# Second conv matrix of a hybrid decoder layer: half of its columns by the seven-product scheme, with three sums of weights made by transfers

## Chip, cores and metric

One NeuronCore of one Trainium2 chip. The metric is the device time of one execution in microseconds (us), as the median of several runs. Of the kernel before there are three runs, from 1184.03 to 1184.84 us, median 1184.58 us.

## What is computed

One layer over 256 tokens (and 16 learned ones in front of them), width D = 2048, all in float32. The part that matters here is the mixer's second branch and what follows it:

```python
u = rms_norm(h, g_pre_mix[l])
z_pool, v_conv, g_conv, gate_a, gate_b = jnp.split(u @ w_in[l], splits, axis=-1)
y_a = causal_multiscale_pool(z_pool, ...) @ w_pool_out[l]
y_b = conformer_conv(v_conv, g_conv, ...) @ w_conv_out[l]      # (256 x 1024) @ (1024 x 2048)
m = jax.nn.sigmoid(gate_a) * y_a + jax.nn.sigmoid(gate_b) * y_b
h = h + rms_norm(m @ w_o[l], g_post_mix[l])
# then the two matrices of the MLP, w_up (2048 x 8192) and w_down (8192 x 2048)
```

`w_conv_out` is the matrix of the change. Only its product is computed in another way.

## The kernel before, in words

**Products.** Every float32 matrix product is made of three rounded ones: an operand is split into a high part (`hi`, a cast on ScalarE, ACT in the profile) and the rest (`lo`, a subtraction on VectorE, DVE), and TensorE (PE) adds hi·hi, hi·lo and lo·hi in PSUM. A *block* of a product is 128 tokens by 512 inner rows by 512 columns: 4 inner tiles times 3 matmuls of 128x512, 12 in all.

**Weights.** A *chunk* is 512 inner rows by 512 columns of a matrix, 1 MB, 128x2048 on chip. `stream` lists the chunks in the order of use. `fetch()` (L296 of the kernel before) keeps two chunks ahead of the one in use: it loads each by a DMA on SyncE's queue (SP) into one of three rooms `raw`, and splits it with one ACT cast (L276) and one DVE subtraction (L279) into one of three pairs of rooms `hi`, `lo`. A room of `hi` and `lo` is free when PE has done the chunk of three places before. A room of `raw` is free when DVE has done its `lo`.

**Stages.** In order of time: the first projection (conv inputs, pool input, gates), the pool's second matrix (`acc_po`), **the conv's second matrix** (`acc_co`, L958 to L962), the matrix `w_o` (`o_a`, `o_b`, `o_c`), and the MLP (`acc_up`, `bank_u`, `bank_a`, `bank_b`). `w_o` and the MLP already use the seven-product scheme, and there `Plan` sets the order of the work. In the stages before `w_o` there is no planner: each engine executes in the order in which the code is written.

**The conv's second matrix before.** `project_t` (L807) takes its 8 chunks one after the other: for each of 4 column blocks `n` two chunks, each used for both token tiles `t` (16 blocks, 192 matmuls). When a column block is done, `evac_conv` (L935) makes `mts` of it for each `t` on DVE: times the gate (L938), plus the pool branch (L939). *Two units later* `feature_steps` (L913) turns `mts` for the next matrix: 4 transposes on PE into a PSUM tile `mt` (L920), the high part `m<-mt` on ACT (L924), the low part `m<-mt,m` on DVE (L927), and for the columns `n` < 2 a copy `A<-mt` on ACT (L929), which is made after the low part of the same tile. There are two rooms for `mt`, so the third tile's transposes wait for the first one's copy. `sums_of_m` (L949) makes four sums of `A` on DVE for the scheme in `w_o`.

**Rooms that matter.** `u` (the projections' input, tag `um` and `ux`) is last read at the end of the gates; then `m` takes the room `um`. `y` and `s_act` (the inputs of the pool's and the conv's second matrix) take two rooms with the tag `k8`, and `early_sums` (two sums of blocks of `w_o`, made by four DMAs on GpSimd's queue, POOL, two of which add) takes `y`'s room after the pool matrix.

Of the kernel before, what the change touches and what calls it, by code (L numbers as in the profile page):

```python
# [15 lines left out]
P = 128  # L16
# [99 lines left out]
def hybrid_block(ctx: ExitStack, tc: tile.TileContext, ins: dict, out: bass.AP):  # L116
# [127 lines left out]
    def part_tile(tag, n, standing=False):  # L244

        key = f"{tag}{n % 3}"
        room = ready.pop(key) if key in ready else part_room(key, f"{tag}_{n}")
        place = 2 if standing and tag == "hi" else 1
        shift = (place - 1 - 3 * KEYS.index(key)) % 4 * LINE
        return room[:, shift:shift + CK * CW]  # L250

    def open_chunk(loads=None):

        n = at["n"]
        at["n"] += 1
        src, (rows, width) = stream[n]
        raw = raws.tile([P, CK * CW], F32, tag="raw", name=f"raw_{n}")
        hi, lo = (part_tile(tag, at["parts"], n in standing_chunks) for tag in ("hi", "lo"))
        at["parts"] += 1
        flat, (raw, hi, lo) = raw, (t.rearrange("p (k c) -> p k c", k=rows) for t in (raw, hi, lo))  # L260
        if n < FIRST:
            dst = raw.rearrange("p k (h c) -> p k h c", h=2)
            for load in loads or [(slice(i, i + 2), BOTH, nc.sync) for i in range(0, rows, 2)]:
                if callable(load):
                    load()
                    continue
                sl, halves_, queue = load
                for k in range(sl.start, sl.stop):
                    queue.dma_start(dst[:, k, halves_], src[:, k, halves_])
        else:  # L270
            nc.sync.dma_start(raw, src)
        pieces = rows if n < FIRST else 4 if n == FIRST else 1
        k = rows // pieces

        def high(sl, cs):
            nc.scalar.copy(hi[:, sl, cs], raw[:, sl, cs])  # L276

        def low(sl, cs):
            nc.vector.tensor_sub(lo[:, sl, cs], raw[:, sl, cs], f32(hi[:, sl, cs]))  # L279
# [10 lines left out]
        opened.append((hi, lo, todo, flat))  # L290

    def split_pieces(c):
        while opened[c][2]:
# [529 lines left out]
    def block(n):  # L823
        return slice(n * CW, (n + 1) * CW)
# [56 lines left out]

    def ln_act():
        a_, b_ = ln_items(0), ln_items(QW)
        pending[0:0] = [a_[0], b_[0], FETCH, a_[1], b_[1], FETCH, a_[2], b_[2]]
    pending += [(0, ln_out), (0, ln_act)]

    def evac_pool(n):
        def f(t, acc):
# [15 lines left out]
    for keys, op in ((((0, 0), (0, 1)), {}), (((0, 1), (1, 1)), {"accum_op": ALU.add})):  # L904
        for e, key in enumerate(keys):
            nc.gpsimd.dma_start(early_sums[:, e].rearrange("p (k c) -> p k c", k=CK),
                                source_o(key), **op)

    pairs_room = big.tile([P, 3, 2 * T], F32, tag="ux", name="pairs")
    m = big.tile([P, LINE + KD * 2 * T], F32R, tag="um", name="m")[:, LINE:].rearrange(  # L910
        "p (k a t) -> p k a t", k=KD, a=2)

    def feature_steps(n, t, mt):  # L913

        box = {}

        def turn():
            box["pt"] = pt = misc_tile(f"mt_{n}_{t}").rearrange("p (k c) -> p k c", k=CK)
            for i in range(CK):
                nc.tensor.transpose(pt[:, i, :], mt[:, i * P:(i + 1) * P], ident)  # L920
        dst = m[:, n * CK:(n + 1) * CK, :, t * P:(t + 1) * P]

        def high():
            nc.scalar.copy(dst[:, :, 0, :], box["pt"])  # L924

        def low():
            nc.vector.tensor_sub(dst[:, :, 1, :], box["pt"], f32(dst[:, :, 0, :]))  # L927
            if n < 2:
                nc.scalar.copy(A[:, t, n], box["pt"])  # L929
        return turn, high, low  # L930

    def mt_of(n, t):
        return mts[:, (n * NT + t) % (CC // CW * 2), :]

    def evac_conv(n):  # L935
        def f(t, acc):
            mt = mt_of(n, t)
            nc.vector.tensor_mul(mt, acc, sg[1][:, t, block(n)])  # L938
            nc.vector.tensor_add(mt, mt, sg[0][:, t, block(n)])  # L939
            blocks.extend(feature_steps(n, t, mt))  # L940
        return f

    def s_act_of(k):
        return ln["out"][:, k, :, :]


    A = big.tile([P, NT, 2, CK, P], F32, tag="a", name="A")

    def sums_of_m():  # L949

        a11, a12, a21, a22 = (A[:, t, h] for t in range(2) for h in range(2))
        nc.vector.tensor_sub(a11, a11, a21)
        nc.vector.tensor_sub(a21, a21, a22)
        nc.vector.scalar_tensor_tensor(a22, a11, -1.0, a22, op0=ALU.mult, op1=ALU.subtract)
        nc.vector.tensor_add(a12, a12, a22)

    mts = big.tile([P, CC // CW * 2, CW], F32, tag="c", name="mts")
# [1115 lines left out]
```

## Time and profile before

| | |
|---|---|
| median of 3 runs | 1184.58 us |
| the profiled execution | 1184.32 us, of which 1182.6 us are its span |
| matmuls' busy share of the span | 99% |
| busy in the conv stage (376.6 to 422.8 us) | PE 46.2 us, DVE 33.5, ACT 20.6 |
| a block of 12 matmuls | 2.72 us |
| a chunk's split | ACT 1.9 us, then DVE 2.3 us |

Times in the trace count from the start of the span. A row of its timeline gives the start, the duration, the engine, the source line and the operation, and in brackets how long the engine was idle before and who released it. PE's matmuls overlap (each lasts 0.39 us, and one starts every 0.227 us), so PE's pace is read from starts.

### The profile page before, as it was taken

The page shows a single profiled execution, that of the slowest core. Times are in us where ns is not written, and L with a number is a line of the kernel's source. Part 1 is how long each engine was busy: PE and PEld are TensorE (multiplying, and loading weights), DVE is VectorE, ACT ScalarE, POOL GpSimd, SP SyncE. Part 2 cuts the span into 40 slices and gives each one's busy share as a digit, 9 for nine tenths or more (in the row PEclk, how much of TensorE's full clock was granted, in tenths as well). Part 3 has the DMA queues.
Part 4 walks back from the last instruction along what each step waited for, and adds up shares of the span by engine and source line. Part 5 has one row for each costly group of instructions (what it writes and reads, how often), then busy time and mean ns, then how long its engine had stood idle before and what let it go on. Part 6 is the DMA issues. An engine that isn't in the chain of part 4 may idle for free.

```text
span 1182.6 us, 15774 instructions
## 1 busy us (share of the span) xinstructions
PE 1172.7 (99%) x6351; PEld 1018.9 (86%) x6351; DVE 1027.6 (87%) x1095; ACT 679.6 (57%) x690; POOL 45.0 (4%) x51
## 2 busy tenths in 40 slices
PE   9999999999999999999999999999999999999997
PEld 9999988888888888898888888888888888888886
DVE  6899978999766799987998988989989989889865
ACT  6533344444584465756566766666656667666642
POOL 1000000000000001000001001000000010010000
PEclk9999999999999999999999999999999999999998
DMA  8655565655647967859869898988998898998861
GB/s 295 214 178 179 182 204 184 196 195 184 208 143 268 265 215 221 290 168 317 248 213 249 228 288 220 269 269 226 281 293 215 267 279 229 282 241 239 303 214 72
DMA packets 177882, 272.91 MB, mean 231 GB/s; under 512 B 4657, under 2 KB 92913, under 8 KB 176912
## 3 DMA queue, kind: packets, MB, share of 16 engines
q1 hardware_dynamic: 160176, 235.88, 59.0%
q0 software_dynamic: 16736, 34.76, 16.2%
q10 hardware_dynamic: 896, 1.25, 0.3%
q8 instruction: 50, 0.82, 0.3%
q14 instruction: 24, 0.20, 0.1%
HBM read 267.68 MB, written 4.19 MB: 230 GB/s over the span
## 4 chain that ended last, share of the span: by engine, by line
PE 99%; DVE 0%; DVEq 0%; issue 0%; ACT 0%; ACTq 0%
PE bank_u L498 18%; PE acc_gate L802 15%; PE bank_a L1787 10%; PE bank_u L504 9%; PE acc_up L1787 8%; PE bank_b L1787 7%; PE o_c L1170 6%; PE acc_z L493 4%; PE acc_co L802 4%; PE acc_po L802 4%; PE acc_v L493 3%; PE acc_g L493 3%; PE acc_vg L493 2%; PE acc_up L498 1%; PE bank_u L1787 1%; PE o_b L1170 1%
## 5 line engine op out<-in xcount | busy, mean ns | idle before, releaser
L498 PE MATMUL bank_u<-m,hi 128*128 128x512 f32 x960 | 329.4, 390 | 0.0
L504 PE MATMUL bank_u<-m,lo 128*128 128x256 f32 x960 | 265.5, 277 | 0.0
L276 ACT CAST hi<-raw 128x2048 fp32r<-128x2048 f32 (+2 forms) x94 | 151.0, 1620 | 188.1 <-PE acc_gate L802 64.0
L498 PEld LDWEIGHTS bank_u<-m,hi 128*128 128x128 f32 x960 | 180.2, 188 | 37.9
L279 DVE TENSOR_TENSOR lo<-raw,hi 128x2048 fp32r<-128x2048 f32 (+2 forms) x94 | 180.0, 1925 | 34.6 <-ACT hi L276 34.1
L1570 DVE TENSOR_TENSOR lo<-raw_m,hi 128x2048 fp32r<-128x2048 f32 x70 | 160.3, 2290 | 31.6 <-ACT hi L1566 31.5
L504 PEld LDWEIGHTS bank_u<-m,lo 128*128 128x128 f32 x960 | 180.3, 188 | 1.4
L1566 ACT CAST hi<-raw_m 128x2048 fp32r<-128x2048 f32 x70 | 133.9, 1912 | 73.7 <-DVE raw_m L1583 21.3
L802 PE MATMUL acc_gate<-hi,u_um 128*128 128x512 f32 x416 | 131.1, 389 | 0.0
L559 DVE SCALAR_TENSOR_TENSOR c<-a,taps,c 128x256 f32<-128x256 f32 x240 | 115.7, 484 | 6.8
L1787 PE MATMUL bank_a<-hi,forms 128*128 128x512 f32 (+1 forms) x288 | 93.5, 386 | 0.0
L802 PEld LDWEIGHTS acc_gate<-hi,u_um 128*128 128x128 f32 x416 | 78.1, 188 | 16.1
L802 PE MATMUL acc_gate<-lo,u_um 128*128 128x512 f32 x208 | 80.9, 389 | 0.0
L1570 DVE TENSOR_TENSOR lo<-raw_a,hi 128x2048 fp32r<-128x2048 f32 x29 | 66.4, 2290 | 10.8 <-ACT hi L1566 10.7
L1566 ACT CAST hi<-raw_a 128x2048 fp32r<-128x2048 f32 x29 | 55.4, 1910 | 35.4 <-PE bank_u L498 13.2
L1566 ACT CAST hi<-raw_c 128x2048 fp32r<-128x2048 f32 x27 | 51.5, 1909 | 27.2 <-PE bank_u L498 12.4
L1570 DVE TENSOR_TENSOR lo<-raw_c,hi 128x2048 fp32r<-128x2048 f32 x27 | 61.8, 2289 | 5.7 <-ACT hi L1566 5.6
L1787 PEld LDWEIGHTS bank_a<-hi,forms 128*128 128x128 f32 x288 | 53.9, 188 | 11.0
L1570 DVE TENSOR_TENSOR fourth_pair<-raw_m,fourth_pair 128x2048 fp32r<-128x2048 f32 x26 | 59.5, 2288 | 4.4 <-ACT fourth_pair L1566 4.4
L1650 ACT COPY half<-bank_u 128x256 f32<-128x256 f32 x60 | 22.2, 370 | 66.0 <-PE bank_u L504 66.0
L1787 PE MATMUL acc_up<-hi,forms 128*128 128x512 f32 x176 | 57.4, 390 | 0.0
L1787 PE MATMUL bank_a<-lo,forms 128*128 128x512 f32 (+1 forms) x144 | 55.6, 386 | 0.0
(419 smaller groups left out, 2265.0 us busy)
## 6 DMA issues: line engine op xcount, KB each, us to landing
raw<-in_w_in_dram SPq DMA_DIRECT2D x52, 1024.0 KB, 5.1
raw_m<-in_w_down_dram SPq DMA_DIRECT2D x38, 1024.0 KB, 7.0
raw_m<-in_w_down_dram POOLq DMA_DIRECT2D x22, 1024.0 KB, 10.6
raw_a<-in_w_up_dram SPq DMA_DIRECT2D x20, 1024.0 KB, 6.4
raw_c<-in_w_up_dram SPq DMA_DIRECT2D x19, 1024.0 KB, 6.9
raw_m<-in_w_up_dram SPq DMA_DIRECT2D x19, 1024.0 KB, 6.9
raw_a<-in_w_down_dram SPq DMA_DIRECT2D x13, 1024.0 KB, 7.3
raw_c<-in_w_down_dram SPq DMA_DIRECT2D x13, 1024.0 KB, 7.3
```

What stands on the lines that cost most here:

```text
L276: nc.scalar.copy(hi[:, sl, cs], raw[:, sl, cs])
L279: nc.vector.tensor_sub(lo[:, sl, cs], raw[:, sl, cs], f32(hi[:, sl, cs]))
L493: nc.tensor.matmul(acc, w[:, k[0], cs], act[:, k[1], a, off:], start=first and n == 0, stop=last and n == 2)
L498: nc.tensor.matmul(acc.rearrange("p (a t) -> p a t", a=2)[:, :, ts], hi[:, k[0], cs], act[:, k[1], :, off + ts.start:off + ts.stop], start ...
L504: nc.tensor.matmul(acc[:, :T], lo[:, k[0], cs], act[:, k[1], 0, off:], start=False, stop=stop, skip_group_check=True)
L559: nc.vector.scalar_tensor_tensor(c, conv["a"][:, q, i:i + T], taps[:, q, i:i + 1], c, op0=ALU.mult, op1=ALU.add)
L802: nc.tensor.matmul(acc, act(kk)[:, a_, ts_], w_[:, k, :], start=kk == 0 and n == 0, stop=kk == nk - 1 and n == 2)
L1170: nc.tensor.matmul(acc, form(k, a_), box[w_][:, k, :], start=start and k == 0 and n == 0, stop=stop and k == CK - 1 and n == 2, skip_group ...
L1566: nc.scalar.copy(box["hi"], raw)
L1570: nc.vector.tensor_sub(box["lo"], raw, f32(box["hi"]))
L1650: nc.scalar.copy(box[j], accs[j][:, :T])
L1787: nc.tensor.matmul(acc, forms[h][:, f, k, a_, :], box[w_][:, k, cs], start=start and k == 0 and n == 0, stop=stop and k == KH - 1 and n == ...
```

## The change

The first 1024 columns of `w_conv_out` (a matrix of 2 by 2 blocks, with 2 by 2 blocks of tokens and inner rows on the other side) are computed with 7 products of blocks instead of 8; the other 1024 columns stay plain. So there are 15 *units* of 12 matmuls instead of 16, written out in the order

`1 5 2 6 X20a X20b 7 3 4 X21a X21b X30a X30b X31a X31b`

where the digits are the scheme's products and `X20a` is column block 2, inner half 0, token tile 0. Each of the products 1 to 7 has a chunk of its own, each `X..` chunk serves two units, so there are 11 chunks to split instead of 8: 65 (unit 1), 66 (5), 67 (2), 68 (6), 69 (X20), 70 (7), 71 (3), 72 (4), 73 (X21), 74 (X30), 75 (X31); before, they were 65 to 72. Chunks 76 to 78 belong to `w_o`.

* **Sums of weights.** Chunks 66, 70 and 72 are sums of two or four blocks of the matrix. Eight DMAs on POOL's queue (three plain, five that add) make them in a new tile `conv_wide` in the room `um`, from the end of the gates on. Chunk 68 is made on DVE: 66 plus one raw block (L318).
* **Sums of activations.** `conv_sums` (four DVE operations, in the pool stage) and four pairs of high and low parts, `conv_forms_0` (pool stage) and `conv_forms_1` (in `y`'s room, so after the pool stage).
* **Sums of results.** Unit 1, 6, 7 and 4 add into one PSUM bank (`chain`), which ACT copies out after 1, 6 and 7; 5 and 3 share a bank (also copied out after 5); three DVE sums make the four results.
* **Order.** `behind(unit)` writes out the evacuations. The features of the first 1024 columns now come behind units 4 (two tiles), X21a and X30a, those of column block 2 behind X30b and X31a.
* `early_sums` starts at unit 4 instead of the stage's start.

DVE's instructions from the gate of the last of the first four results to the gate of column block 2, after (`lo_75`, `lo_76` are splits of chunks, `mt_0_0`, `mt_1_1`, `mt_1_0`, `mt_0_1` the PSUM tiles of column block and token tile, the rows on `A` alone are `sums_of_m`):

```order
L1038 TENSOR_TENSOR mts_3397<-mts_3397,sg0_1829 128x512
L998 TENSOR_TENSOR m_3544<-mt_0_0_3572,m_3544 128x4x128
L998 TENSOR_TENSOR m_3544<-mt_1_1_3580,m_3544 128x4x128
L293 TENSOR_TENSOR lo_75_3590<-raw_75_3588,hi_75_3589 128x2048
L998 TENSOR_TENSOR m_3544<-mt_1_0_3606,m_3544 128x4x128
L293 TENSOR_TENSOR lo_76_3628<-raw_76_3626,hi_76_3627 128x2048
L998 TENSOR_TENSOR m_3544<-mt_0_1_3645,m_3544 128x4x128
L1013 TENSOR_TENSOR A_3479<-A_3479 128x512
L1014 TENSOR_TENSOR A_3479<-A_3479 128x512
L1015 SCALAR_TENSOR_TENSOR A_3479<-A_3479 128x512
L1016 TENSOR_TENSOR A_3479<-A_3479 128x512
L1037 TENSOR_TENSOR mts_3397<-acc_co_2a_3480,sg1_2414 128x512
```

Before, the same kind of work around `sums_of_m` on DVE:

```order
L927 TENSOR_TENSOR m_3377<-mt_1_0_3560,m_3377 128x4x128
L927 TENSOR_TENSOR m_3377<-mt_1_1_3568,m_3377 128x4x128
L952 TENSOR_TENSOR A_3378<-A_3378 128x512
L953 TENSOR_TENSOR A_3378<-A_3378 128x512
L954 SCALAR_TENSOR_TENSOR A_3378<-A_3378 128x512
L955 TENSOR_TENSOR A_3378<-A_3378 128x512
L279 TENSOR_TENSOR lo_72_3582<-raw_72_3580,hi_72_3581 128x2048
L938 TENSOR_TENSOR mts_3379<-acc_co2_0_3528,sg1_2414 128x512
```

Two splits now stand between the low parts of `mt`, and all of it stands ahead of the gate of column block 2.

ACT's instructions in the same place, after:

```order
L995 CAST m_3544<-mt_0_0_3572 128x4x128
L1000 COPY A_3479<-mt_0_0_3572 128x512
L995 CAST m_3544<-mt_1_1_3580 128x4x128
L1000 COPY A_3479<-mt_1_1_3580 128x512
L290 CAST hi_75_3589<-raw_75_3588 128x2048
L995 CAST m_3544<-mt_1_0_3606 128x4x128
L1000 COPY A_3479<-mt_1_0_3606 128x512
L290 CAST hi_76_3627<-raw_76_3626 128x2048
L995 CAST m_3544<-mt_0_1_3645 128x4x128
L1000 COPY A_3479<-mt_0_1_3645 128x512
```

and before:

```order
L924 CAST m_3377<-mt_1_0_3560 128x4x128
L929 COPY A_3378<-mt_1_0_3560 128x512
L924 CAST m_3377<-mt_1_1_3568 128x4x128
L929 COPY A_3378<-mt_1_1_3568 128x512
L276 CAST hi_72_3581<-raw_72_3580 128x2048
L276 CAST hi_73_3617<-raw_73_3616 128x2048
L924 CAST m_3377<-mt_2_0_3646 128x4x128
```

Before, two casts of chunks followed the last copy of a column block; now one stands behind each second copy. On PE the transposes of one tile stand between two units, after (end of X30b, `mt_2_0`, begin of X31a):

```order
L1105 MATMUL acc_co_3b_3661<-lo_74_3550,s_act_3118 128x512
L1105 MATMUL acc_co_3b_3661<-hi_74_3549,s_act_3118 128x512
L991 MATMUL mt_2_0_3674<-ident_88,mts_3397 128x128 x4
L1105 MATMUL acc_co_3a_3632<-hi_75_3589,s_act_3118 128x512
L1105 MATMUL acc_co_3a_3632<-lo_75_3590,s_act_3118 128x512
```

The transposes read the `mts` that the last row of DVE's list above begins to make. Before, the transposes of a column block's two tiles stood together, two units behind its last matmul; now each tile's stand alone, those of column block 2 three units behind its last matmul.

The diff, cut:

```diff
-    for w, nk in ((w_pool_out, KP), (w_conv_out, KC)):
-        for n in range(NB):
-            stream += columns(w, 0, nk, n * CW)
+    for n in range(NB):
+        stream += columns(w_pool_out, 0, KP, n * CW)
...
+    CONV = ("1", "5", "2", "6", "X20", "7", "3", "4", "X21", "X30", "X31")
...
+    def open_room(key):
+
+        raw = conv_raw(key)
+        hi, lo = (part_tile(tag, at["parts"]) for tag in ("hi", "lo"))
+        at["parts"] += 1
+
+        more = conv_raw("3") if key == "5" else None
+
+        def f():
+            nc.scalar.copy(hi, raw)
+            nc.vector.tensor_sub(lo, raw, f32(hi))
+            if more is not None:
+                nc.vector.tensor_add(raw, raw, more)
...
+    conv_wide = big.tile([P, 3, CK * CW], F32, tag="um", name="conv_wide")
+
+    sums_ = {"6": ((0, 0), (0, 1)), "7": ((0, 1), (1, 1)), "4": ((0, 0), (0, 1), (1, 1), (1, 0))}
+    for i in range(4):
+        for n, (key, blocks_) in enumerate(sums_.items()):
+            conv_rooms[key] = conv_wide[:, n]
+            if i < len(blocks_):
+                add_into(conv_rooms[key], conv_block(*blocks_[i]), ALU.add if i else None)
...
+    def behind(unit):
+
+        if unit == "1":
+            nc.scalar.copy(held[0, 0], chain)
...
+        elif unit == "3":
+            nc.vector.tensor_sub(held[1, 0], with_3, held[1, 0])
+            gate_conv(1, 0)
+        elif unit == "4":
+            gate_conv(0, 1, chain)
+            features(0, 0)
+            features(1, 1)
+        elif unit == "X21a":
+            features(1, 0)
+        elif unit == "X30a":
+            features(0, 1)
+            sums_of_m()
+            gate_conv(2, 0, acc_of["2a"])
+            gate_conv(2, 1, acc_of["2b"])
+        elif unit == "X30b":
+            features(2, 0)
+        elif unit == "X31a":
+            features(2, 1)
+            gate_conv(3, 0, acc_of["3a"])
+        elif unit == "X31b":
+            gate_conv(3, 1, acc_of["3b"])
...
+    for unit in UNITS:
+        if unit[-1] != "b":
+            hi, lo = fetch()
...
-    blocks = []
-    for n in range(NB):
-        after += blocks + [sums_of_m] * (n == 2)
-        blocks.clear()
-        project_t(s_act_of, KC, evac_conv(n), f"co{n}")
```

More of the change, by code (lines that the diff above doesn't have):

```diff
@@ L255, in open_chunk @@
         at["n"] += 1
-        src, (rows, width) = stream[n]
+        src, shape = stream[n]
+        if src is None:
+            open_room(shape)
+            return
+        rows, width = shape
         raw = raws.tile([P, CK * CW], F32, tag="raw", name=f"raw_{n}")
@@ L933, in mt_of @@
         return mts[:, (n * NT + t) % (CC // CW * 2), :]
[L935 to L941, printed above, removed]
     def s_act_of(k):
         return ln["out"][:, k, :, :]
-    A = big.tile([P, NT, 2, CK, P], F32, tag="a", name="A")
     def sums_of_m():
@@ new lines, in hybrid_block @@
+    hi = lo = None
+    for unit in UNITS:
+        if unit[-1] != "b":
+            hi, lo = fetch()
+        if unit == "X20a":
+            A = big.tile([P, NT, 2, CK, P], F32, tag="a", name="A")
+        if unit == "4":
+            for keys, op in ((((0, 0), (0, 1)), {}), (((0, 1), (1, 1)), {"accum_op": ALU.add})):
+                for e, key in enumerate(keys):
+                    nc.gpsimd.dma_start(early_sums[:, e].rearrange("p (k c) -> p k c", k=CK),
+                                        source_o(key), **op)
+        key = unit if unit[0] != "X" else unit[1] + unit[3]
+        kb = 0
+        if unit[0] == "X":
+            t, kb = "ab".index(unit[3]), int(unit[2])
+            if not kb:
+                acc_of[key] = acc_tile(f"acc_co_{key}")
+            form = lambda k, a_: s_act_of(kb * CK + k)[:, a_, t * P:(t + 1) * P]
+        else:
+            form = conv_form(unit)
+        acc = acc_of.get(key, chain)
+        start = unit in ("1", "2", "5") or unit[0] == "X" and not kb
+        for k in range(CK):
+            for n, (a_, w_) in enumerate(((0, hi), (0, lo), (1, hi))):
+                nc.tensor.matmul(acc, form(k, a_), w_[:, k, :], start=start and k == 0 and n == 0,
+                                 stop=k == CK - 1 and n == 2, skip_group_check=True)
+        if unit == "3":
+            m = big.tile([P, LINE + KD * 2 * T], F32R, tag="um", name="m")[:, LINE:].rearrange(
+                "p (k a t) -> p k a t", k=KD, a=2)
+        behind(unit)
```

79 lines of the change are left out of this document (72 added, 7 removed).

## Prediction, made before the changed kernel was run

> **What bounds the kernel now.** First the page: the busy line and the chain that ended last.
>
> ```profile
> PE 1172.7 (99%) x6351; PEld 1018.9 (86%) x6351; DVE 1027.6 (87%) x1095; ACT 679.6 (57%) x690; POOL 45.0 (4%) x51
> ```
> ```profile
> PE 99%; DVE 0%; DVEq 0%; issue 0%; ACT 0%; ACTq 0%
> ```
>
> The chain is TensorE from end to end: each us of PE work removed, and each us in which PE waits, goes straight into the time. Next the conv stage, in the table of windows, the chain and PE's timeline:
>
> ```profile
> 376.60:422.80 46.20, 46.20 (x217) 38.50 (x216) 33.52 (x32) 20.58 (x18) 4.16 (x4) 1.00 0.84 251
> ```
> ```profile
> 376.74 16.32 PE acc_co L802 x72
> ```
> ```profile
> 376.57 0.39 PE L802 MATMUL acc_co<-hi,s_act 128*128 128x512 f32 x1
> ```
> ```profile
> 392.90 1.03 PE L920 MATMUL mt<-ident,mts 128*128 128x128 f32 x8
> 393.69 0.47 PE L802 MATMUL acc_co<-hi,s_act 128*128 128x512 f32 x1
> ...
> 422.83 0.39 PE L1170 MATMUL o_c<-hi,m 128*128 128x512 f32 x1
> ```
>
> PE is busy throughout, DVE 33.5 of 46.2 us. 72 matmuls are six blocks: 16.32/6 = 2.72 us for a unit. Eight transposes take 0.79 us by starts; as the first matmul behind them is longer too, I take 0.44 for one tile's four. The stage runs from 376.57 to 422.83.
>
> **What the change removes.** One block, 2.72 us of PE.
>
> **What it adds beside PE.** Three more splits, the sum for chunk 68, four sums of activations, four forms and three sums of results: on DVE 3 x 2.2 + 2.2 + (4 + 4 + 3) x 0.65, about 16 us, of which some 4 lie in the pool stage. 33.5 + 12 = 45.5 us, in a stage that would last 43.5. So the question is which order they have. The prices, from DVE's timeline:
>
> ```profile
> 362.40 2.29 DVE L279 TENSOR_TENSOR lo<-raw,hi 128x2048 fp32r<-128x2048 f32 x1 [0.77 <-ACT hi L276]
> ```
> ```profile
> 373.28 2.29 DVE L279 TENSOR_TENSOR lo<-raw,hi 128x2048 fp32r<-128x2048 f32 x1 [3.15 <-ACT hi L276]
> ...
> 401.35 0.68 DVE L938 TENSOR_TENSOR mts<-acc_co,sg 128x512 f32<-128x512 f32 x1
> 402.06 0.69 DVE L939 TENSOR_TENSOR mts<-mts,sg 128x512 f32<-128x512 f32 x1
> 402.67 0.69 DVE L938 TENSOR_TENSOR mts<-acc_co,sg 128x512 f32<-128x512 f32 x1
> ...
> 404.00 2.29 DVE L279 TENSOR_TENSOR lo<-raw,hi 128x2048 fp32r<-128x2048 f32 x1
> 406.20 0.68 DVE L927 TENSOR_TENSOR m<-mt,m 128x512 fp32r<-128x512 f32 x1
> 408.03 0.69 DVE L927 TENSOR_TENSOR m<-mt,m 128x512 fp32r<-128x512 f32 x1 [1.14 <-ACT m L924]
> 408.63 0.68 DVE L952 TENSOR_TENSOR A<-A 128x512 f32<-128x512 f32 x1
> ...
> 411.48 2.29 DVE L279 TENSOR_TENSOR lo<-raw,hi 128x2048 fp32r<-128x2048 f32 x1
> ```
>
> By starts: a `lo` 2.2 us, a 512-wide operation 0.61, or 0.72 if the next needs its result; the four sums of `A` 2.8. From ACT's:
>
> ```profile
> 382.21 1.91 ACT L276 CAST hi<-raw 128x2048 fp32r<-128x2048 f32 x1 [3.53 <-PE acc_co L802]
> ...
> 406.92 0.59 ACT L929 COPY A<-mt 128x512 f32<-128x512 f32 x1 [0.99 <-DVE m L927]
> 407.40 0.59 ACT L924 CAST m<-mt 128x512 fp32r<-128x512 f32 x1
> 408.75 0.59 ACT L929 COPY A<-mt 128x512 f32<-128x512 f32 x1 [0.76 <-DVE m L927]
> 409.23 3.97 ACT L276 CAST hi<-raw 128x2048 fp32r<-128x2048 f32 x2
> ```
>
> A cast of a chunk takes 1.91 and starts 0.20 after the unit that frees its room (376.57 + 2 x 2.72 = 382.01, then 382.21). The copy `A<-mt` starts 0.72 after its `m<-mt,m` (408.03 to 408.75), so it **waits for DVE**, and what follows on ACT starts 0.48 later.
>
> **The early units.** The window of the pool stage, and the first cast that waits for its end:
>
> ```profile
> 333.00:376.60 43.60, 43.60 (x195) 36.09 (x194) 31.32 (x26) 27.61 (x30) 0.00 (x0) 1.00 0.58 192
> ```
> ```profile
> 376.77 1.91 ACT L276 CAST hi<-raw 128x2048 fp32r<-128x2048 f32 x1 [2.01 <-PE acc_po L802]
> ```
>
> There DVE works 31.3 of PE's 43.6 us, so `conv_sums` and the first forms (some 4 us) cost nothing, and `lo_66` stands at 373.28, as the split of that number does now. The second forms need `y`'s room, so ACT casts them from 376.77 on, 2 x 0.48, and `hi_67` follows from 377.7 to 379.6. DVE has the sum for chunk 68 (2.2) behind `lo_66` (2.2), two gates of the pool (1.2) and the second forms' low parts (1.2), then `lo_67`, from 380.2 to 382.5. Unit 2 starts at 376.57 + 5.44 = 382.01 and needs `lo` in its second matmul, at 382.24: PE waits 0.3. Units 6, X20a and X20b are in time. Call E the end of X20b: 376.57 + 6 x 2.72 + 0.3 = 393.2.
>
> **The chain behind E.** Chunk 72 takes the rooms of chunk 69, which X20b is the last to use. So its cast starts at E + 0.2 and `lo_72` at E + 2.1, and from there DVE has no gap: `lo_72`, sum and gate of (1,1) (2.05), `lo_73`, sum and gate of (1,0) (2.05), `lo_74`, gate of (0,1) (1.33). That is 3 x 2.2 + 5.4 = 12.0, so `m<-mt_0_0,m` starts at E + 14.2. Behind it ACT and DVE take turns, as the two lists of the order show:
> * `m<-mt_1_1,m` 1.83 later (the step 406.20 to 408.03), E + 16.0; its copy `A` + 0.72; `hi_75` + 0.48, done 1.91 later, E + 19.1;
> * `lo_75` 2.2, `m<-mt_1_0,m` at E + 21.4; `A` + 0.72; `hi_76` + 0.48, done at E + 24.5;
> * `lo_76` 2.2, `m<-mt_0_1,m` at E + 26.7; `A` + 0.72, done + 0.6, E + 28.0;
> * the four sums of `A`, which need that copy, 2.8; the gate of (2,0) 1.4: E + 32.3. Then PE may start `mt_2_0`.
>
> PE's own work from E to that place is units 7, 3, 4, X21a, X21b, X30a and X30b, 7 x 2.72, and four tiles' transposes, 1.75: 20.8 us. It is there 11.5 us early. Part of that wait falls earlier: after X21a (E + 11.75) `mt_1_0` needs the room of `mt_0_0`, whose copy ends at E + 15.5, so PE waits 3.8 there and 7.7 ahead of `mt_2_0`. Queued behind are X31a and X31b, which have their weights, and all of `w_o`.
>
> From `mt_2_0` to the first matmul of `w_o` there are 2 x 2.72 + 2 x 0.44 = 6.3 us: E + 38.6 = 431.8, where it was 422.83. **+9.0 us.** From there on the order is as before, and so is the state: the last gate still waits for the last unit, `hi_78` for its room, and they stand as far behind `w_o`'s first matmul as now.
>
> **The clock.** After 7.7 us of waiting PE may not go on at full pace. The rows nearest to it are the first ones of the execution:
>
> ```profile
> 1.12 3.35 PE L394 MATMUL idle<-rb 128*128 128x128 f32 x14 [1.12 <-DVE rb L308]
> 4.27 0.63 PE L410 MATMUL xm<-ident,m_rows 128*128 128x128 f32 x2
> ...
> 5.66 0.83 PE L394 MATMUL idle<-rb 128*128 128x128 f32 x6
> 6.42 0.25 PE L600 MATMUL idle<-row_ssq,rows_of 128*16 128x1 f32 x4
> ```
>
> The same matmul took (4.27 - 1.12)/14 = 0.225 us from rest and (6.42 - 5.66)/6 = 0.127 two us later, though the granted clock of the page reads full there. A restart like that costs 14 x 0.098 = 1.4 us; bounds 0 and 1.8 (by the 0.1 of a transpose in place of 0.127). I take 1.4, as the nearest row. After the first wait it would be hidden in the second.
>
> The Trainium skill, "TensorE: Matmul & The Clock Gate", section "Part 1: The HAM clock gate (the "warmup" mystery)", says that TensorE falls to half its clock after about 3.4 us without work and is back after as long under load. By that rule a restart would cost 1.7 us, an estimate from that page. The rows of the start agree in kind; no run here shows it within a kernel.
>
> **The transfers.** The eight sums' DMAs start when the gates are done with `u`, at 325. The gate's matmuls on it, the loads of 320 to 460, the issues of 376 to 402 (where `early_sums` makes two such chains), and the landing of its four:
>
> ```profile
> L802 PE MATMUL acc_gate<-hi,u_um x416: 388/389/401, 152.6 to 325.0; 128*128 128x512 f32 x139
> ```
> ```profile
> raw<-in_w_pool_out_dram SPq DMA_DIRECT2D x6, 1024.0 KB, 5.1
> ```
> ```profile
> raw<-in_w_conv_out_dram SPq DMA_DIRECT2D x3, 1024.0 KB, 13.3
> ```
> ```profile
> DMA to landing us min/median/max: 7.4/11.8/18.0
> ```
>
> An adding transfer takes up to 18 us, and loads beside two of them 13.3 where they take 5.1 alone. Chunk 72 is the longest chain: one plain and three that add, 325 + 9 + 3 x 18 = 388 at most; its cast is due at 393.4. The sums are in time; the loads beside them are the risk. In the pool stage each load leaves 8 to 12 us ahead of its cast, and each cast stands several us ahead of PE. `raw_67` leaves when `lo_64` is done: now that starts at 362.4, after 0.8 of idle time, and ends at 364.6; with `conv_sums` (2.8) and the first forms (1.2) ahead of it, at 367.8. It is wanted at 377.7: with 5.1 it is there, with 13.3 it is some 3.5 late, and unit 2 with it. I take 0, since by then only one adding transfer is left of three; the other end is 3.5. The loads of chunks 73 to 77 leave when DVE frees their rooms, 15 us or more ahead of their casts in the chain above. `early_sums`, moved to unit 4 (its room is free at about 399), ends by 399 + 9 + 18 = 426, and `w_o` wants it some 3 us after its start: nothing.
>
> **Sum.** Against the profiled execution, 1184.32 us (1182.6 of span and 1.7 around it): + 9.0 (that is 11.7 of waits less 2.72) + 1.4 = 1194.7. The median of the runs shown is 0.3 above that execution, which is less than I can tell.
>
> **Rivals.**
> * *The block is saved* (6%): DVE and ACT keep ahead, PE never waits, 1184.3 - 2.7 = 1181.6, faster. It decides at the gate of (2,0): it would have to be done at E + 20.8 instead of E + 32.3, which takes the two splits 75 and 76 (each cast and `lo`, 4.1 us and more) out of its chain. For it speaks that DVE has 12.7 us free in the stage now; against it, the order.
> * *The clock stays up* (20%): 1193.3. For it, the granted clock's column; against it, the first rows.
> * *Loads late* (14%): unit 2 waits 3.5 longer, and E and all behind it shifts: 1198.2. For it the 13.3; against it that the chains overlap and mostly end before.
> * That the change doesn't remove the block is excluded: PE's list after it has 15 units of 12 matmuls.
> * In 5% the early part of the chain is covered otherwise and the waits about equal the block: near 1185.
>
> The forecast itself has 55%. Range 1191.5 to 1199: below the clock's rival by a chain 6% shorter, above the late loads by the bound of the clock. Faster by over 0.2% (2.4 us, about what a measurement of this kernel can tell from no change) 7%, within 4%, slower 89%.
>
> **What would show it.** In the changed trace PE should stand idle just twice, ahead of `mt_1_0` for about 4 us and ahead of `mt_2_0` for 7 to 8, released by ACT's `A` and by DVE's `mts`; DVE should have no idle time from `lo_72` to `m<-mt_0_0,m`; the first matmuls after the second wait should be spaced wider than 0.227; `w_o` should begin near 433. Wrong would be: PE without a gap behind X21a (then DVE was not the limit), a wait of ACT's cast of chunk 67 for its DMA, or a `conv_wide` transfer that lands after 393.

## The result, and the profile after

The changed kernel takes **1197.53 us** (median of 4 runs, 1196.6 to 1197.84) where the kernel before takes 1184.57 on the same chip: a ratio of 1.0109, 95% interval 1.0091 to 1.0126. The forecast was 1194.7, range 1191.5 to 1199. The profiled execution took 1197.84 us with a span of 1196.1, so 13.5 more than the one of before.

The page's busy line and its chain, then the conv stage in the table of windows (span, busy time of PE, PEld, DVE, ACT and POOL, granted clock, DMA share, GB/s):

```profile
PE 1176.6 (98%) x6339; PEld 1020.9 (85%) x6339; DVE 1043.9 (87%) x1110; ACT 689.3 (58%) x701; POOL 54.0 (5%) x59
```
```profile
PE 93%; DVE 3%; DMA 2%; ACT 1%; issue 0%; DVEq 0%; ACTq 0%
```
```profile
377.70:436.50 58.80, 49.44 (x205) 39.92 (x204) 46.78 (x43) 29.34 (x27) 4.44 (x5) 0.88 0.76 220
```

PE has 12 matmuls fewer (6351 to 6339), but the stage takes 58.8 us instead of 46.2, and PE is busy in 49.4 of them. DVE, ACT and DMA now stand in the chain that was PE from end to end. Moreover the 49.4 is more than 15 units at 2.72 and the transposes of 6 tiles at 0.44 (43.4 together): in part of the stage PE is slower, and the granted clock of the window is 0.88.

The table of waits shows for what PE stands idle (us in total, times, longest), and its timeline when (start, duration, in brackets the idle time ahead and what ended it):

```profile
PE mt L991 <- DVE mts L1038: 5.0, 1, 5.0
PE mt L991 <- ACT A L1000: 3.6, 1, 3.6
PE acc_co_with L1105 <- DVE lo L293: 0.8, 1, 0.8
PE acc_po L844 <- DVE lo L293: 0.6, 1, 0.6
```
```profile
377.69 0.39 PE L1105 MATMUL acc_co_chain<-hi,s_act 128*128 128x512 f32 x1
...
384.31 0.50 PE L1105 MATMUL acc_co_with<-lo,s_act 128*128 128x512 f32 x1 [0.80 <-DVE lo L293]
...
395.10 0.39 PE L1105 MATMUL acc_co_chain<-hi,conv_forms 128*128 128x512 f32 x1
...
410.65 1.12 PE L991 MATMUL mt<-ident,mts 128*128 128x128 f32 x4 [3.59 <-ACT A L1000]
411.41 0.78 PE L1105 MATMUL acc_co_2b<-hi,s_act 128*128 128x512 f32 x1
...
427.50 1.09 PE L991 MATMUL mt<-ident,mts 128*128 128x128 f32 x4 [4.98 <-DVE mts L1038]
...
436.55 0.39 PE L1318 MATMUL o_c<-hi,m 128*128 128x512 f32 x1
```

The stage starts 1.1 us later than before (377.69, 376.57); 0.25 of this was there at the gates' first matmul already (152.90, 152.65), far ahead of the change. E, the start of unit 7, is at 395.10. There are two long waits, ahead of `mt_1_0` and `mt_2_0`, and `w_o` begins at 436.55 instead of 422.83: +13.7, where the whole execution is 13.5 longer. So the loss lies ahead of `w_o`.

The chain behind E on DVE and on ACT:

```profile
397.24 2.29 DVE L316 TENSOR_TENSOR lo<-conv_wide,hi 128x2048 fp32r<-128x2048 f32 x1 [1.62 <-ACT hi L315]
...
409.29 0.68 DVE L998 TENSOR_TENSOR m<-mt,m 128x512 fp32r<-128x512 f32 x1
411.11 0.69 DVE L998 TENSOR_TENSOR m<-mt,m 128x512 fp32r<-128x512 f32 x1 [1.14 <-ACT m L995]
414.25 2.29 DVE L293 TENSOR_TENSOR lo<-raw,hi 128x2048 fp32r<-128x2048 f32 x1 [2.45 <-ACT hi L290]
416.46 0.68 DVE L998 TENSOR_TENSOR m<-mt,m 128x512 fp32r<-128x512 f32 x1
419.61 2.29 DVE L293 TENSOR_TENSOR lo<-raw,hi 128x2048 fp32r<-128x2048 f32 x1 [2.46 <-ACT hi L290]
...
423.15 0.69 DVE L1013 TENSOR_TENSOR A<-A 128x512 f32<-128x512 f32 x1 [0.65 <-ACT A L1000]
...
425.94 0.68 DVE L1037 TENSOR_TENSOR mts<-acc_co_2a,sg 128x512 f32<-128x512 f32 x1
426.66 0.69 DVE L1038 TENSOR_TENSOR mts<-mts,sg 128x512 f32<-128x512 f32 x1
```
```profile
410.01 0.59 ACT L1000 COPY A<-mt 128x512 f32<-128x512 f32 x1 [5.52 <-DVE m L998]
...
412.32 1.90 ACT L290 CAST hi<-raw 128x2048 fp32r<-128x2048 f32 x1
...
417.18 0.59 ACT L1000 COPY A<-mt 128x512 f32<-128x512 f32 x1 [2.47 <-DVE m L998]
417.66 1.91 ACT L290 CAST hi<-raw 128x2048 fp32r<-128x2048 f32 x1
```

Read against E = 395.10, these are the steps of the forecast: `m<-mt_0_0,m` at E + 14.2, `lo_75` at E + 19.15, `lo_76` at E + 24.5, the gate of (2,0) done at 427.35, E + 32.25. Each engine's brackets name the other one. ACT's copy of `A` waits for DVE's `m`, the cast behind it starts 0.48 later, and DVE then stands 2.45 us until that cast is done. In a stage where PE waits 9 us, DVE thus stands idle too: it isn't full there, it is held by the order.

Two things came out larger than forecast. One is the loss of pace behind each wait, in the chain of after (start, duration) and in the windows:

```profile
428.58 4.92 PE acc_co_3a L1105 x12
433.51 0.44 PE mt L991 x4
433.94 2.76 PE acc_co_3b L1105 x12
```
```profile
411.00:421.00 10.00, 10.00 (x39) 8.17 (x38) 4.98 (x4) 5.93 (x7) 0.46 (x1) 0.75 1.10 256
427.40:437.00 9.60, 9.50 (x35) 7.79 (x35) 6.46 (x8) 3.18 (x4) 0.00 (x0) 0.70 0.03 11
```

A unit of 12 matmuls takes 4.92 us right behind the second wait and 2.76 one unit later. Cut closer, the windows show the granted clock at 0.50 in two stretches (it is 1.00 from 405.80 to 409.20, from 416.10 to 426.25 and from 433.15 to 440):

```profile
409.25:416.05 6.80, 5.40 (x15) 4.45 (x16) 3.21 (x4) 3.94 (x5) 1.27 (x1) 0.50 1.07 270
426.35:433.10 6.75, 5.60 (x16) 4.57 (x17) 5.01 (x6) 2.38 (x2) 0.00 (x0) 0.50 0.21 59
```

Both begin before PE goes on. The second ends 5.6 us after PE's restart at 427.50, and PE loses about half of these, 2.75. The other thing is the transfers, from the same chain in the pool stage:

```profile
343.22 19.31 DMA raw<-in_w_pool_out_dram
...
366.87 10.40 DMA raw_conv<-in_w_conv_out_dram
```

A load that takes 5.1 us alone took 19.3 beside the sums' transfers, and PE waited 0.6 us for it ahead of the stage.

### The profile page after: what moved, and what is told of

Same layout as the page of the kernel before. It is cut to its first block, busy times and chain, and to the rows that moved or that the text cites. A ratio compares the mean times of both kernels' runs of the same rounds, so it can differ in the third digit from the quotient of the medians.

```text
span 1196.1 us, 15791 instructions
## 1 busy us (share of the span) xinstructions
PE 1176.6 (98%) x6339; PEld 1020.9 (85%) x6339; DVE 1043.9 (87%) x1110; ACT 689.3 (58%) x701; POOL 54.0 (5%) x59
## 3 DMA queue, kind: packets, MB, share of 16 engines
q0 software_dynamic: 20192, 43.15, 19.3%
## 4 chain that ended last, share of the span: by engine, by line
PE 93%; DVE 3%; DMA 2%; ACT 1%; issue 0%; DVEq 0%; ACTq 0%
PE bank_u L540 18%; PE acc_gate L844 15%; PE bank_a L1935 10%; PE bank_u L546 9%; PE acc_up L1935 8%; PE bank_b L1935 7%; PE o_c L1318 5%; PE acc_z L535 4%; PE acc_v L535 3%; PE acc_g L535 3%; PE acc_vg L535 2%; DMA raw<-in_w_pool_out_dram 2%; PE acc_up L540 1%; DVE lo L293 1%; PE bank_u L1935 1%; DMA raw_conv<-in_w_conv_out_dram 1%
## 5 line engine op out<-in xcount | busy, mean ns | idle before, releaser
L290 ACT CAST hi<-raw 128x2048 fp32r<-128x2048 f32 (+2 forms) x92 | 147.2, 1613 | 177.5 <-PE acc_gate L844 64.0
L293 DVE TENSOR_TENSOR lo<-raw,hi 128x2048 fp32r<-128x2048 f32 (+2 forms) x92 | 175.4, 1917 | 30.2 <-ACT hi L290 29.8
```

## The experiments

Theory: the order on DVE and ACT behind E makes both waits, PE's slow pace behind them comes from its having stood still, and the transfers that add make the loads ahead of E late. Rivals: the volume of DVE's and ACT's work, in whatever order; separate causes for the two waits; contention with transfers or other engines as the cause of the slow pace. The kernel before took 1184.13 to 1184.57 us beside these runs. Where nothing else is said, a run is the changed kernel with the edit shown.

### The gate ahead of the split

```diff
+        elif unit == "X21b":
+            gate_conv(2, 0, acc_of["2a"])
         elif unit == "X30a":
             features(0, 1)
-            sums_of_m()
-            gate_conv(2, 0, acc_of["2a"])
             gate_conv(2, 1, acc_of["2b"])
+            sums_of_m()
```

> The gate of (2,0) moves from behind the four sums of A to directly behind m<-mt_1_0,m, ahead of the split of chunk 76; the four sums move behind the gate of (2,1). Nothing else changes. Theory of the order (the gate is late because two splits, a copy and the sums stand ahead of it): the gate is done at E + 21.4 + 0.7 + 1.4 = E + 23.5, PE comes to mt_2_0 at about E + 27.2 with its slow stretch after the first wait, so the second wait (5.0 us) and the slow pace behind it (2.7) go: 1197.5 - 7.7 = 1189.8; the first wait stays at 3.6. Theory of the volume (VectorE and ScalarE simply have too much to do in this stage, in whatever order): the wait comes back ahead of mt_0_1, mt_2_1 or w_o, and the time stays within 2 us of 1197.5.

Measured 1190.47 us (1.0052, 1.0037 to 1.0067). PE's timeline around the old places of the waits:

```profile
410.35 0.66 PE L991 MATMUL mt<-ident,mts 128*128 128x128 f32 x4 [3.58 <-ACT A L1000]
...
421.19 0.60 PE L991 MATMUL mt<-ident,mts 128*128 128x128 f32 x4
```

The first wait stays as it was, the second is gone; `w_o` begins at 427.62, and only two waits of 0.7 come back in it. That is 7.1 us by the places of a gate and of the four sums, with the amount of work unchanged: the order, as far as this wait goes.

### PE kept busy through both waits

```diff
         elif unit == "X21a":
+            idle_work(14)
             features(1, 0)
...
         elif unit == "X30b":
+            idle_work(32)
             features(2, 0)
```

`idle_work(n)` issues n matmuls of 128x512 into `with_2`, which nothing reads any more.

> 46 idle matmuls of 128x512 into a bank that nothing reads any more, 14 ahead of mt_1_0 and 32 ahead of mt_2_0, so that PE works through both waits (3.2 and 7.3 us of the 3.6 and 7.6). Theory of the clock (X21b took 5.0 us and X31a 4.9 instead of 2.72 because PE had stood still): X21b, X31a and the transposes are back at 0.227 a matmul; the first gain is eaten by a longer second wait, the second counts: 1197.5 - 2.7 = 1194.8. If the slow pace comes from something else in that stretch (transfers, contention for the banks): the matmuls stay slow and the time stays at 1197.5 or rises by what the idle matmuls overshoot.

Measured 1194.75 us (1.0090, 1.0073 to 1.0106). The same two windows as of the changed kernel above:

```profile
411.00:421.00 10.00, 10.00 (x47) 8.25 (x47) 5.08 (x4) 5.75 (x6) 0.03 (x1) 1.00 1.09 252
427.40:437.00 9.60, 9.60 (x50) 8.02 (x49) 8.27 (x10) 5.92 (x6) 0.00 (x0) 1.00 0.10 11
```

The granted clock is 1.00 in both, the DMA's traffic in the first is the same (1.09 and 252 GB/s against 1.10 and 256), and from `mt_2_0` to `w_o` it is 6.4 us (427.20 to 433.62) instead of 9.05. So the slow pace comes from having stood still and not from the traffic, and it costs 2.8 us in all.

### The copy ahead of the low part

```diff
         def high():
             nc.scalar.copy(dst[:, :, 0, :], box["pt"])
+            if n < 2:
+                nc.scalar.copy(A[:, t, n], box["pt"])
...
             nc.vector.tensor_sub(dst[:, :, 1, :], box["pt"], f32(dst[:, :, 0, :]))
-            if n < 2:
-                nc.scalar.copy(A[:, t, n], box["pt"])
```

> The copy A<-mt is written ahead of m<-mt,m instead of behind it, so ScalarE no longer waits for VectorE there and VectorE waits for ScalarE. Theory of taking turns: hi_75 starts at about E + 11.4 instead of E + 17.2, lo_75 stands right behind m<-mt_1_1,m, hi_76 is then held by its room (the end of X21b) instead; the gate of (2,0) is done near E + 29.8 instead of E + 32.3, so the second wait falls from 5.0 to between 2.5 and 3.3: 1195.0, or 1192.3 if such a short wait leaves the clock up. Without that coupling (VectorE's own row of work is the limit): no change of more than 0.5.

Measured 1192.15 us (1.0065, 1.0050 to 1.0080). ACT, and the two waits of PE:

```profile
405.01 0.62 ACT L997 COPY A<-mt 128x512 f32<-128x512 f32 x1
405.49 1.94 ACT L290 CAST hi<-raw 128x2048 fp32r<-128x2048 f32 x1
```
```profile
409.69 0.66 PE L991 MATMUL mt<-ident,mts 128*128 128x128 f32 x4 [2.96 <-DVE m L1000]
...
423.97 1.09 PE L991 MATMUL mt<-ident,mts 128*128 128x128 f32 x4 [3.35 <-DVE mts L1038]
```

`hi_75` starts at 405.5 instead of 412.3. Both waits get shorter, to 3.0 and 3.3. The median is near the second number of the expectation, but not for its reason: the clock did drop in the profiled execution, for a shorter stretch (from X31a's first matmul to the transposes behind it 4.06 us, where it was 5.11), and that execution took 1193.14. The four runs lie from 1190.49 to 1193.21, so that agreement is partly luck.

### The first tile earlier

```diff
             gate_conv(1, 0)
+            features(0, 0)
         elif unit == "4":
             gate_conv(0, 1, chain)
-            features(0, 0)
             features(1, 1)
```

> The transposes, cast and low part of tile (0,0) stand behind unit 3 instead of unit 4, so that on VectorE m<-mt_0_0,m comes ahead of lo_74 and of the gate of (0,1). This takes away the first of PE's two waits alone. Theory of the one chain (both waits are the same lateness, and only the gate of (2,0) sets the end): the first wait (3.6 us) goes to about 0 and X21b is back at 2.7, but the gate of (2,0) is only some 0.8 earlier (no wait of 1.14 between the two m, one m already done), so the second wait grows from 5.0 to about 10: 1196.7. If the two waits are separate costs: 1197.5 - 3.6 = 1193.9 or less.

Measured 1197.97 us (1.0115, 1.0099 to 1.0130): no gain. PE, and DVE at `lo_74`:

```profile
429.37 1.09 PE L991 MATMUL mt<-ident,mts 128*128 128x128 f32 x4 [11.56 <-DVE mts L1038]
```
```profile
409.45 2.29 DVE L293 TENSOR_TENSOR lo<-raw,hi 128x2048 fp32r<-128x2048 f32 x1 [2.46 <-ACT hi L290]
```

The first wait is gone but for 0.5 us ahead of X30a, and the rest stands ahead of `mt_2_0`: 11.6 us, as much as the forecast's 11.5 for both together. The waits are one lateness, of the gate of (2,0). PE may start `mt_2_0` 33.7 us after E instead of 32.4, since `A<-mt_0_0` now stands ahead of `hi_74` on ACT and DVE waits 2.46 for that cast.

### The order mended as a whole

Three of the edits above together (the gate of (2,0) behind X21b, the copy first, tile (0,0) behind unit 3), and `sums_of_m` behind the gate of (3,1).

> All the edits of the order together: tile (0,0) behind unit 3, A<-mt ahead of m<-mt,m, the gate of (2,0) behind X21b, the four sums of A behind the gate of (3,1). The amount of work is that of the changed kernel. Theory of the order: counted from E the gate of (2,0) is done at E + 19.6 and PE comes there at E + 20.8, so neither wait remains, the clock stays up, and w_o begins at E + 27.2 = 422.3 instead of 436.5: 1197.5 - 14.2 = 1183.3, about 1 us under the kernel before (the block saved, 2.7, less what is late ahead of E, 1.9). Theory of the volume: 3 us or more of waits stay ahead of mt_2_1, mt_3_0 or w_o, 1186.5 or more.

Measured 1190.45 us (1.0054, 1.0041 to 1.0066), 7 above the expectation of 1183.3. Up to `w_o` it was met: PE has no wait from E (395.02) to `w_o`, which begins at 422.50. The work is that of the changed kernel, so in the conv stage the rival of the volume is out. Then, on PE and in the chain that ended last:

```profile
428.62 0.63 PE L991 MATMUL mt<-ident,mts 128*128 128x128 f32 x4 [3.24 <-DVE mts L1038]
```
```profile
408.60 13.64 DMA raw<-in_w_o_dram
```

Chunk 77, which `w_o` needs second, takes 13.6 us to load, since `early_sums`, whose room is held by the second forms up to unit 3, is now transferred at the same time (issued from 400.9 to 411). In the changed kernel that load takes 13.7 us too, but `w_o` begins 14 us later, and PE doesn't wait for it. So the theory of the order holds for the conv stage, and neither theory had the load.

### Transfers that only overwrite

```diff
-                add_into(conv_rooms[key], conv_block(*blocks_[i]), ALU.add if i else None)
+                add_into(conv_rooms[key], conv_block(*blocks_[i]), None)
```

This kernel leaves the sums of weights out: the three chunks hold the block that came last.

> The eight transfers into conv_wide stay, with the same bytes and order, but none adds: each overwrites, so the second matrix is computed with other weights than it should be. Theory of the late loads (a load beside adding transfers takes 10 to 19 us instead of 5, which shifts E by 1.6 us of the 1.9): the casts of chunk 63 and 67 no longer wait for their DMA, PE's waits of 0.6 and 0.8 go, E comes back to about 393.5 and the time to 1197.5 - 1.6 = 1195.9. If bytes alone make the loads late and not the adding: no change, 1197.5.

Measured 1195.26 us (1.0093, 1.0077 to 1.0108). The same window of the changed kernel and of this one:

```profile
340.00:366.00 26.00, 26.00 (x117) 21.47 (x115) 18.46 (x17) 18.18 (x24) 1.98 (x2) 1.00 1.09 274
```
```profile
340.00:366.00 26.00, 26.00 (x117) 21.52 (x116) 20.56 (x19) 19.78 (x26) 2.25 (x3) 1.00 1.02 374
```

With the DMA engines as busy (1.02 and 1.09) they move 374 GB/s without the adding and 274 with it. The early waits of PE go but for 0.15 us in unit 2, and E comes to the forecast's 393.2:

```profile
393.14 0.39 PE L1105 MATMUL acc_co_chain<-hi,conv_forms 128*128 128x512 f32 x1
```

The time falls by 2.3, and E comes 1.96 earlier. 0.4 of that were there at the gates' first matmul already (152.47, 152.90), so 1.5 are the adding's: it makes the loads late.

### The transfers in another order

First 6, 4, 6+, 4+, 4+, 7, 4+, 7+ in place of 6, 7, 4, 6+, 7+, 4+, 4+, 4+, on the changed kernel:

> The eight transfers into conv_wide keep their bytes and their adding; only the order in which GpSimd issues them changes: 6, 4, 6+, 4+, 4+, 7, 4+, 7+ in place of 6, 7, 4, 6+, 7+, 4+, 4+, 4+, so that two chains instead of three are under way at a time. If it is the three adding at once that make the loads late: the waits of 0.6 and 0.8 go as in the run with plain transfers, 1195.5. If it is the bytes that adding moves, whenever they come: the loads of the pool's chunks stay late and the time stays within 0.7 of 1197.5.

Measured 1202.25 us (1.0151, 1.0137 to 1.0165), worse than either expectation (1195.5, and within 0.7 of 1197.5). The loads of the pool's chunks did come in time, but the last two adding transfers now leave at 369.0 and 372.9, and the load of chunk 67 leaves at 368.5:

```profile
368.50 15.39 DMA raw<-in_w_conv_out_dram
```

Unit 2 waits 4.8 us for it (3.1 and 1.7) instead of 0.8. With the mended order as well:

> The mended order of the chain and the new order of the transfers together. If both theories hold, the gains add: 1183.3 - 2 = 1181.3, 0.26% under the kernel before; if the order of the transfers does nothing, 1183.3 as with the mended order alone.

Measured 1195.88 us (1.0098, 1.0084 to 1.0112), 12.6 above the higher of its two expectations (1181.3 and 1183.3): 4.2 us of waits in unit 2, 5.1 in `w_o`. PE's waits between E and `w_o` are gone, the loss of the transfers is there. In both runs the lateness went to another load beside the adding.

### Early sums later, the third chain last

On the mended order. First, the transfers into `early_sums` behind the loads of chunks 76 and 77:

```diff
-        if unit == "4":
-            for keys, op in ((((0, 0), (0, 1)), {}), (((0, 1), (1, 1)), {"accum_op": ALU.add})):
+        if unit == "X31a":
+            for queue, keys, op in ((nc.sync, ((0, 0), (0, 1)), {}),
+                                    (nc.gpsimd, ((0, 1), (1, 1)), {"accum_op": ALU.add})):
...
```

> The mended order (e6) with one more edit: the four transfers into early_sums are issued behind the loads of w_o's first two chunks, the two plain ones on the queue of the loads, the two that add on GpSimd's, and not at unit 4 any more. In e6 w_o began at 422.5 as forecast, and then PE waited 3.2 + 0.7 + 0.9 because the load of chunk 77 took 13.6 us beside the four transfers. Theory of the loads beside adding transfers: chunk 77 is there by 415, these waits and the slow pace behind the first of them (1.1) go: 1190.45 - 5.9 = 1184.5. If the stage has too much to load in any order: the wait comes back at raw_o or early_sums in w_o, 1187 or more.

Measured 1186.95 us (1.0027, 1.0016 to 1.0038), 2.5 above the expectation. Chunk 77 is in time and `w_o` begins at 422.05 and goes on, but PE waits 1.5 and 1.6 later in it, for DVE and for a load of `raw_o` of 11.5 us. In addition, the third chain behind the other two (6, 7, 6+, 7+, 4, 4+, 4+, 4+):

> As e9, and the eight transfers into conv_wide in the order 6, 7, 6+, 7+, 4, 4+, 4+, 4+: the third chain starts behind the first two. If three chains at once are what makes the loads of the pool stage late, E comes back by up to 1.9: 1182.6. If it is the bytes that adding moves beside the loads, the lateness only moves to other loads, as in e7: 1184.5 give or take 2.

Measured 1185.51 us (1.0013, 1.0004 to 1.0021). And, in place of that, none of the eight transfers into `conv_wide` adds (the two into `early_sums` still do):

> As e9, but none of the eight transfers into conv_wide adds (each overwrites, the second matrix is computed with other weights). It shows what the change would give if its sums of weights cost the loads nothing: E at about 393.4 and no wait in the conv stage, so 1184.5 - 2.2 = 1182.3, which is 2.1 below the kernel before: most of the block's 2.72.

Measured 1185.55 us (1.0012, 1.0003 to 1.0021). Both are some 3 us above their expectations (1182.6 and 1182.3), which saw no wait in `w_o`. With the third chain last, E is at 393.00 and there is no wait ahead of `w_o`, as without adding (393.11): for the loads ahead of E this order of the transfers is as good as no adding. PE with the third chain last:

```profile
420.48 0.39 PE L1318 MATMUL o_c<-hi,m 128*128 128x512 f32 x1
```
```profile
PE o_c L1318 <- DVE lo L1271: 1.7, 1, 1.7
PE o_a L1318 <- DVE m L998: 1.6, 1, 1.6
```
```profile
395.20:431.80 36.60, 35.03 (x170) 28.68 (x169) 36.18 (x37) 22.22 (x24) 2.54 (x2) 1.00 0.86 256
```

`w_o` begins 2.35 us *earlier* than in the kernel before: here most of the saved block is seen (2.0 of it; 0.33 was there at the stage's start already, 376.24 and 376.57). It is given back inside `w_o`, with 3.3 us of idle time in two waits: one for a load of `raw_o` that takes 11.5 us beside the adding transfers into `early_sums`, one for DVE. DVE is busy for 36.2 of the 36.6 us up to `m<-mt_3`, so its volume may be the limit there, once the order is mended.

### The sums of A on GpSimd

On the kernel with the third chain last. The four sums go to GpSimd, behind the gate of (2,1), and the transfers into `early_sums` leave one chunk earlier, at X30a:

```diff
-        nc.vector.tensor_sub(a11, a11, a21)
-        nc.vector.tensor_sub(a21, a21, a22)
...
+        nc.gpsimd.tensor_sub(a11, a11, a21)
+        nc.gpsimd.tensor_sub(a21, a21, a22)
+        nc.gpsimd.tensor_add(a22, a11, a22)
+        nc.gpsimd.tensor_sub(a12, a12, a22)
+        nc.gpsimd.tensor_scalar_mul(a22, a22, -1.0)
...
```

> As e10, with two edits for its last two waits in w_o (1.6 and 1.7). The four sums of A go from VectorE, which in e10 has no gap from 395.2 to 431.8, to GpSimd (five operations there, as the negated sum takes two), behind the gate of (2,1) in the program; and the plain transfers into early_sums leave behind the load of chunk 76 instead of 77, the adding ones behind them. Theory of the volume as what is left once the order is mended: VectorE's last lines come 2.8 earlier, m<-mt_3 is done before o_a needs it, the first wait goes; the second goes if raw_o's load is not beside adding transfers any more. 1185.5 - 3.3 = 1182.2, or 1183.9 if only the first goes. Rival: GpSimd's operations slow VectorE's beside them, or are themselves late for forms_o; then 1185.5 or more.

Measured 1185.19 us (1.0010, 1.0001 to 1.0019), not to be told from the last two, and still 1.0 above the kernel before. PE's waits fell from 3.3 to 2.6 only. With the transfers into `early_sums` moved ahead (the two that add leave at 410.7 and 414.4 instead of 416.0 and 418.3), another load came late: `raw_o`, issued at 411.6, took 14.0 us, and ACT's cast of it waited 5.6. The wait ahead of `o_a` stayed at 1.6, now behind that load and no longer behind a full DVE, which stood 2.1 us for the cast. So that DVE's volume is the limit in `w_o` is not shown. None of the twelve kernels is faster than the one before: the lateness of loads in `w_o` was moved, not removed.

## Why the prediction was right, point by point

* **The block removed**, 2.72: as forecast.
* **Unit 2**, 0.3 of waiting: 0.8 of idle time measured, 1.1 by PE's starts, since `lo_67` was late.
* **E at 393.2**: 395.10. The step that failed is that of the transfers, "I take 0": 1.1 us were lost before the stage began (0.25 of them ahead of the gates' first matmul, where no such transfer runs yet) and 0.8 more than the 0.3 within it. The other end, 3.5, was too much. The forecast looked at `raw_67` alone, and its 13.3 was of loads beside two adding chains; here there were three, an adding transfer took up to 24.5 us, and the loads that were late are `raw_63` (19.3 us, where it counted on 8 to 12 us of lead) and `raw_conv`. A sign that the forecast had named as one of being wrong, a wait of ACT's cast of chunk 67 for its DMA, was there, 0.9 us. The run without adding shows the cause.
* **The chain behind E**: E + 32.3 forecast, E + 32.25 measured. The moved gate, the moved copy and the mended order show that it was the order. The run with the first tile earlier shows that both waits are one lateness, as the sum had it.
* **The two waits**, 3.8 and 7.7: 3.59 and 4.98. The difference of the second is the slow pace behind the first, 2.6 us (410.65 to 416.4 for four transposes and X21b, 5.8 instead of 3.16), hidden as forecast.
* **The clock**, 1.4 with bounds 0 and 1.8: 2.75 (9.05 from `mt_2_0` to `w_o` instead of 6.3). Here a term was mis-sized, and its bound was too low. The forecast took 14 short transposes' worth of slow pace from the start of the execution; in the stage the granted clock stayed at 0.50 for 5.6 us of work, over four transposes and nearly all 12 matmuls of X31a.
* **`early_sums`**, nothing: right here by luck, because `w_o` began 14 us late; with the order mended, waits of 4.8 in `w_o` came with it, and they shrank to 3.1 when it was moved.
* **After `w_o` begins**, nothing: +13.7 there, +13.5 at the end.

Together: 433.2 forecast for `w_o`'s start, 436.55 measured: 1.9 from E, 0.1 from the chain, 1.35 from the clock. Both misses are on the same side, and the time is nearer to the rival "loads late" (1198.2) than to the forecast's 1194.7; that rival had its cause right and its place, unit 2 alone, only in part. The rival "the block is saved" named the right place for a cure, the gate of (2,0). With the order mended, DVE's 12.7 us free in the stage were enough there: PE had no wait ahead of `w_o`. Then late loads, and perhaps DVE's volume, took the gain in `w_o`.

In the run with the third chain last, the 3.3 us of idle time cost 4.0 by PE's starts (39.34 us for the first 160 matmuls and transposes of `w_o`, where it was 35.35), so 2.35 earlier becomes 1.6 later at the last matmul; its span is 1.3 longer, as the rest behind that matmul is 0.3 shorter. What stays open is what `w_o`'s remaining waits would take: the one further plan of its transfers that was tried, in the last run, made another load late.

## What to carry to other kernels

When TensorE is the bound and a change trades its matmuls for work beside it, write down, for the engines that do that work, the rows in order from the first instruction that is held by a room to the one TensorE waits for, with durations from the trace: here that list was right to 0.1 us, while the sum of busy times (45.5 in 43.5) would have given 2 us for waits of 9. Count a wait of about 3 us together with the slow unit behind it (1.7 and 2.75 us more here), but only the last wait of a chain, as those before it are swallowed. And weight sums made by adding transfers are not free just because GpSimd's queue is idle: loads beside them took up to 19 us instead of 5.1. Their order decides whether PE feels it: in one order the kernel lost 4.7 us, in another the loads ahead of E were as good as without adding.

## What the runs showed of the hardware

**The clock within a kernel.** After a wait of 2.96 us (the copy first) the matmuls behind it were already slow: X21b took 4.4 us (410.11 to 414.53). In the changed kernel, slow matmuls start 0.427 us apart (411.99 to 413.27 for three), 1.88 times 0.227. Behind a wait of 3.58 in the run with the gate moved, the transposes and the first matmuls were at full pace, and only from 411.8, 1.4 us after PE went on, to 415.2 were they slow. The Trainium skill, "TensorE: Matmul & The Clock Gate", section "Part 1: The HAM clock gate (the "warmup" mystery)", says that the clock is judged in windows of about 3.4 us that run freely, and that it drops after an idle one. That the drop can come after the wait's end agrees; that 2.96 us were enough, less than a window, doesn't, and the measurement decides. Within these executions the stretches at 0.50 last 3.4, 6.8 or 10.2 us, whole multiples of 3.4, so the price of a wait seems to depend on where it falls as well as on its length: 2.75 us behind 4.98 in the changed kernel, 1.7 behind 3.35 with the copy first (423.97 to 431.97 instead of 6.3). Nor did PE have to stand still for a whole such stretch. With the gate moved, it was busy for 1.43 of the 3.42 us up to the drop (408.36 to 411.78); with the order and the transfers changed, it was busy for 1.50 of 3.41 (428.49 to 431.90), and the clock stayed at 1.00 until 435.3. Waits of up to 1.7 us in `w_o` (the third chain last) left it at 1.00.

**ACT and DVE at one PSUM tile.** The copy `A<-mt` and `m<-mt,m` only read `mt`, yet ACT's copy waits for DVE's operation when it is written behind it. The Trainium skill, "PSUM — Partial Sum Buffer", section "PSUM bank collisions raise a hardware error", says that the compiler's scheduler puts an order between accesses of two engines to one bank, reads included. The traces agree: ACT waits 5.52 us for DVE in the one order, and with the copy first it doesn't wait. A PSUM tile of its own for each of the two readers wasn't tried.

**GpSimd beside DVE.** The same operation on 128x512 takes DVE 0.69 us and took GpSimd 1.3 to 3.2:

```profile
418.82 1.29 POOL L1013 TENSOR_TENSOR A<-A 128x512 f32<-128x512 f32 x1
420.19 3.23 POOL L1014 TENSOR_TENSOR A<-A 128x512 f32<-128x512 f32 x1
```
```profile
419.57 2.70 DVE L293 TENSOR_TENSOR lo<-raw,hi 128x2048 fp32r<-128x2048 f32 x1 [1.38 <-ACT hi L290]
```

DVE's split beside them took 2.70 instead of 2.29. One such pair is too little to tell more from.
